# Output of the recurrence: row tiles in passes of 4 and 4, sums of squares on TensorE, one inverse root ahead of two norms

## Chip, core and metric

The kernel runs on one core of a Trainium2 chip. The metric is the device time of one execution in microseconds. TensorE multiplies, ScalarE (ACT), VectorE (DVE) and GpSimd (POOL) do the rest, SyncE issues transfers. Each engine executes its own list of instructions in order; an instruction that waits holds up all behind it on its engine. TensorE runs at one of two levels, 1.2 and 2.4 GHz; the profile prints the granted clock as a share of the higher.

## What is computed

A block of two layers (attention, then a recurrent layer of a wkv scan beside a long convolution) on 1024 tokens of width 1024, a root-mean-square norm over its output, and a second block that begins with a norm of its own and a wide input product. What the change touches is the end of the recurrent layer and the two norms in a row:

```python
def rms_norm(x, gain):
    y = x * lax.rsqrt(jnp.mean(x * x, axis=-1, keepdims=True) + 1e-6)
    return y * gain
def rwkv_readout(y, r, k_bonus, v, r_k, gn_w, gn_b):       # group norm of the scan's output per head
    mean = jnp.mean(y, axis=-1, keepdims=True)
    var = jnp.mean(jnp.square(y - mean), axis=-1, keepdims=True)
    yn = (y - mean) * lax.rsqrt(var + 64e-5) * gn_w + gn_b
    return yn + jnp.sum(r * k_bonus * r_k, axis=-1, keepdims=True) * v
# end of rec_layer
y = jnp.concatenate([y_rw * silu(g_rw), y_hy * silu(g_hy)], axis=-1) @ w_out
x = x + gate * y
# end of the first block, start of the second
x = rms_norm(x, final_norm)
h = rms_norm_2(x, g_mix) @ w_in
```

## The kernel before

Activations lie transposed: width on the partitions in 8 tiles of 128 rows, tokens along the free axis in two halves of 512. A float32 product is three reduced-precision matmuls: both operands are split into a rounded part and a remainder (hi, lo), and hi x hi, lo x hi and hi x lo are added up in one PSUM bank. For weights `wblock` does this for each output row tile: a transfer into wf (two buffers), whi on ACT (L273), wlo on DVE or POOL as `self.wlo` says (L274). `dense` runs over the output row tiles m and the token halves and issues the matmuls (L291); a list ks names the row tiles k of the input that take part. `evac` or `evac2` takes a finished bank; what they yield is called again after the next product group. `tick` is called once per product group.

The output product of the recurrence (`rec_layer`, weights rec_w_out) has 8 input row tiles k: in the order of this kernel 0 to 2 and 5 come from the convolution, 3, 4, 6 and 7 from the scan; 7 is the head pair (pair 3) whose scan output still has to go through `rwkv_readout`, a generator of some 24 steps that goes over the two token halves: broadcast of per-head numbers along the partitions (a transpose L245, then selection matmuls L252), mean and variance by small matmuls against a 0/1 matrix (L1878, L1906), an inverse root on DVE, and the scaling (L1895 DVE, L1896 ACT, L1897 POOL, L1898 DVE). `part` splits one row tile (yhi on ACT L412, ylo on DVE L413).

The first pass takes k = 0 to 4 for all m and both halves, adds into x3T (L1968) and ticks the readout one step per product group. Then the rest of the readout runs, row tiles 5 to 7 are split, and the second pass takes k = 5 to 7 for the first half. Its `evac2` adds into x3T (L1972) and calls `squares`: ACT squares the row tile (L359), POOL adds it into x3sq (L360), and DVE adds it, weighted by the square of final_norm, into x3sqg (L366). With both sums at hand, `mix_norm` makes the inverse roots for the two norms at once: four matmuls against ones add up the partitions (`mean_square`, L373), r1 is the inverse root of the first mean, r2 that of the weighted mean times r1 squared, and their product is broadcast over the partitions (`rbc`, L390, copied by ACT L392). `modulate` multiplies (L400 DVE), rounds (L402 ACT) and takes the remainder (L403, DVE or POOL). Then come the second pass of the other half and its `mix_norm`, in block 2, and block 2's input product.

The order on each engine is not that of the code: a scheduler simulates the program and decides it, and tile pools decide what may overlap. So products of one stage stand among those of the next: 48 products of block 2's input on the first half stand ahead of the second half's broadcast.

Of the kernel before, what the change touches and what calls it, by code (L numbers as in the profile page):

```python
# [11 lines left out]
F32 = mybir.dt.float32  # L12
# [129 lines left out]
class Kern:  # L142
# [207 lines left out]
    def squares(self, p, acc, t0, n, x, m, gained=None):  # L350
# [10 lines left out]
        if gained is not None:  # L361
            g, gain = gained[0][:, sl], gained[1]
            if m == 0:
                nc.vector.tensor_scalar(g, sq, gain, None, OP.mult)
            else:
                nc.vector.scalar_tensor_tensor(g, sq, gain, g, OP.mult, OP.add)  # L366
# [666 lines left out]
class KernB(Kern):  # L1033
# [887 lines left out]
    def rec_layer(self, xT, acc, close_x, pools, open_x, d_x, d_out, ahead):  # L1921
# [35 lines left out]
        xo, acc, accg = open_x()  # L1957
        with self.pool(name="b3y", bufs=1) as q:
# [11 lines left out]
            def evac2(m, gi, t0, n, ps):  # L1970
                x = xo[:, m, t0:t0 + n]
                nc.vector.scalar_tensor_tensor(x, ps[:, :n], mod[:, 16 + m, 0:1], x, OP.mult, OP.add)  # L1972
                self.squares(q, acc, t0, n, x, m, (accg, g2[:, m:m + 1]))
                if t0:
                    self.st.dma_start(d_out[m * 128:(m + 1) * 128, :], xo[:, m, :])

            g2 = self.t(self.cst, [128, 8], F32, "fn2")
            nc.vector.tensor_tensor(g2, self.c("final_norm"), self.c("final_norm"), OP.mult)
# [9 lines left out]
            for k in second:  # L1988
                part(k)
# [3 lines left out]
            ahead(xo, acc, accg, *(self.t(s, [128, 8, 512], F32R, n) for s, n in ((yps, "yH"), (yqs, "yB"))), tmp, self.t(q, [128, 1284], F32, "ush2", bufs=1)[:, :512])  # L1993
            self.dense(A["rec_w_out"], list(range(8)), yhi, ylo, LAT[1:], evac2, ks=second)
        self.wlo = nc.vector
        return (wp, yq, yp), (yps, yqs)
# [69 lines left out]
class KernC(KernB):  # L2066
# [507 lines left out]
    def mix_norm(self, x, acc, accg, t0, tmp, rb, hi, lo):  # L2574

        nc = self.nc
        r1 = self.r1[:, t0 // 128:t0 // 128 + 4]
# [176 lines left out]
```

## Time and profile before

| | us |
|---|---|
| median of 3 runs | 4241.47 (4241.17 to 4248.0) |
| the profiled execution: time | 4248.29 |
| its span | 4246.3 |
| TensorE busy | 3869.0 (91%) |
| DVE busy | 2661.3 (63%) |
| ACT busy | 1897.4 (45%) |
| POOL busy | 1231.6 (29%) |
| first rec_w_out product to the second half's broadcast | 2398.91 to 2552.65 |

The mean granted clock was 0.953. The shares are averages over stages with different limits; the change touches a stretch of some 160 us, which is read by windows and timelines of its own. In a timeline a row's "[0.34 <-POOL wlo L274]" says that the engine stood idle for 0.34 us before it and what released it. Neighbouring matmuls overlap, so the time that a matmul takes from the stream is the distance between starts, not the duration in its row.

### The profile page before, as it was taken

The page shows a single profiled execution, that of the slowest core. Times are in us where ns is not written, and L with a number is a line of the kernel's source. Part 1 is how long each engine was busy: PE and PEld are TensorE (multiplying, and loading weights), DVE is VectorE, ACT ScalarE, POOL GpSimd, SP SyncE. Part 2 cuts the span into 40 slices and gives each one's busy share as a digit, 9 for nine tenths or more (in the row PEclk, how much of TensorE's full clock was granted, in tenths as well). Part 3 has the DMA queues.
Part 4 walks back from the last instruction along what each step waited for, and adds up shares of the span by engine and source line. Part 5 has one row for each costly group of instructions (what it writes and reads, how often), then busy time and mean ns, then how long its engine had stood idle before and what let it go on. Part 6 is the DMA issues. An engine that isn't in the chain of part 4 may idle for free. (4 is left out here: it accounts for less than half of the span.)

```text
span 4246.3 us, 68831 instructions
## 1 busy us (share of the span) xinstructions
PE 3869.0 (91%) x25613; PEld 3186.3 (75%) x25613; DVE 2661.3 (63%) x5485; ACT 1897.4 (45%) x4210; POOL 1231.6 (29%) x1300
## 2 busy tenths in 40 slices
PE   7989997899999988968999879989988897999999
PEld 4778886777787767757888757878867786888787
DVE  6741525798834678756673265699777868665532
ACT  6433415777724545415667523334327433333321
POOL 4522302333333533322111043122212126544200
PEclk9999998999999999979999989999999998999999
DMA  6454316431233655564444323324345351222422
GB/s 207 154 177 161 131 70 183 103 90 31 74 119 99 181 147 171 165 163 124 125 121 113 116 88 102 112 87 141 107 128 135 132 179 52 85 80 84 152 102 73
DMA packets 388598, 516.56 MB, mean 122 GB/s; under 512 B 171751, under 2 KB 264823, under 8 KB 386600
## 3 DMA queue, kind: packets, MB, share of 16 engines
q1 hardware_dynamic: 369448, 441.38, 33.9%
q0 software_dynamic: 14064, 53.48, 3.7%
q10 hardware_dynamic: 4752, 17.30, 1.3%
q8 instruction: 202, 3.31, 0.3%
q14 instruction: 132, 1.08, 0.1%
HBM read 348.74 MB, written 164.63 MB: 121 GB/s over the span
## 5 line engine op out<-in xcount | busy, mean ns | idle before, releaser
L291 PE MATMUL bank<-hhi,whi 128*128 128x512 f32 (+1 forms) x1264 | 486.2, 385 | 12.5 <-ACT hhi L405 10.2
L291 PE MATMUL bank<-hlo,whi 128*128 128x512 f32 (+1 forms) x1264 | 483.6, 383 | 3.6 <-DVE hlo L406 1.9
L291 PE MATMUL bank<-hhi,wlo 128*128 128x512 f32 (+1 forms) x1264 | 481.8, 381 | 0.0
L273 ACT ACTIVATE whi<-wf 128x1024 fp32r<-128x1024 f32 (+3 forms) x202 | 193.7, 960 | 455.1 <-PE bank L291 391.3
L274 POOL TENSOR_TENSOR wlo<-wf,whi 128x1024 fp32r<-128x1024 f32 (+1 forms) x96 | 217.0, 2261 | 521.8 <-ACT whi L273 489.6
L291 PEld LDWEIGHTS bank<-hhi,whi 128*128 128x128 f32 x1264 | 243.3, 193 | 60.2 <-ACT hhi L405 11.0
L291 PEld LDWEIGHTS bank<-hlo,whi 128*128 128x128 f32 x1264 | 242.9, 192 | 54.0 <-DVE hlo L406 4.4
L291 PEld LDWEIGHTS bank<-hhi,wlo 128*128 128x128 f32 x1264 | 242.4, 192 | 46.0
L2495 PE MATMUL bank<-th,wh 128*128 128x512 f32 x616 | 246.5, 401 | 6.9 <-ACT th L2420 6.9
L2495 PE MATMUL bank<-th,wl 128*128 128x512 f32 x616 | 247.0, 401 | 0.0
L328 POOL TENSOR_TENSOR walo<-wa,wahi 128x512 fp32r<-128x512 f32 x96 | 130.6, 1375 | 245.2 <-ACT wahi L327 241.6
L417 POOL CAST phi<-split 128x512 fp32r<-128x512 f32 (+1 forms) x104 | 62.8, 604 | 457.9 <-ACT split L416 369.3
L291 PE MATMUL bank<-yT,whi 128*128 128x512 f32 (+1 forms) x600 | 192.9, 390 | 0.9 <-ACT rb L392 0.5
L413 DVE TENSOR_TENSOR plo<-bank,phi 128x512 fp32r<-128x512 f32 (+2 forms) x260 | 167.0, 653 | 37.6 <-ACT phi L412 36.4
L412 ACT ACTIVATE phi<-bank 128x512 fp32r<-128x512 f32 (+2 forms) x260 | 144.5, 568 | 57.1 <-PE bank L730 29.3
L291 PE MATMUL bank<-yH,whi 128*128 128x512 f32 x376 | 153.3, 408 | 11.4 <-ACT ev_a L2158 7.9
L291 PE MATMUL bank<-yB,whi 128*128 128x512 f32 x376 | 151.8, 404 | 7.5 <-DVE yB L403 6.7
L274 DVE TENSOR_TENSOR wlo<-wf,whi 128x1024 fp32r<-128x1024 f32 (+2 forms) x106 | 118.5, 1121 | 54.3 <-ACT whi L273 54.2
L291 PE MATMUL bank<-yH,wlo 128*128 128x512 f32 x376 | 151.8, 404 | 0.8 <-POOL wlo L274 0.7
L2495 PE MATMUL bank<-tl,wh 128*128 128x512 f32 x352 | 142.4, 405 | 5.6 <-DVE tl L2421 4.7
L704 ACT ACTIVATE P<-S,mx 128x768 f32<-128x768 f32 (+7 forms) x144 | 118.2, 822 | 64.9 <-DVE mx L700 58.9
L2495 PEld LDWEIGHTS bank<-th,wh 128*128 128x128 f32 x616 | 117.8, 191 | 37.0 <-ACT th L2420 8.7
(633 smaller groups left out, 11319.7 us busy)
## 6 DMA issues: line engine op xcount, KB each, us to landing
wf<-in_w_in_dram SPq DMA_DIRECT2D x47, 512.0 KB, 3.4
wf<-in_w_ffn_in_dram SPq DMA_DIRECT2D x44, 512.0 KB, 3.6
d_rec<-r_rec SPq DMA_DIRECT2D x40, 512.0 KB, 2.7
wf<-in_rec_w_in_dram ACTq DMA_DIRECT2D x33, 512.0 KB, 4.2
wf<-in_attn_w_in_dram SPq DMA_DIRECT2D x26, 512.0 KB, 3.8
wa<-in_attn_ada_w_dram POOLq DMA_DIRECT2D x24, 512.0 KB, 3.9
wa<-in_rec_ada_w_dram POOLq DMA_DIRECT2D x24, 512.0 KB, 4.1
LK<-d_rec SPq DMA_DIRECT2D x64, 192.0 KB, 3.5
```

What stands on the lines that cost most here:

```text
L273: nc.scalar.activation(hi, wf, AF.Copy)
L274: self.wlo.tensor_tensor(lo, wf, hi, OP.subtract)
L291: self.mark = nc.tensor.matmul(ps[:, :n], w[:, k - k0, :], x(k, t0, n), start=(k == ks[0] and j == 0), stop=(k == ks[-1] and j == 2))
L328: nc.gpsimd.tensor_tensor(lo[:, k], w3[:, k], hi[:, k], OP.subtract)
L412: nc.scalar.activation(hi, src, AF.Copy)
L413: nc.vector.tensor_tensor(lo, src, hi, OP.subtract)
L417: nc.gpsimd.tensor_copy(hi, full)
L704: nc.scalar.activation(P[:, :at], S[:, :at], AF.Exp, bias=m[:, i:i + 1], scale=-1.0, accum_out=st["rs"][:, bi, u["h"]:u["h"] + 1])
L2495: self.mark = nc.tensor.matmul(ps, w[i][:, k, :], x[i][k], start=(k == 0 and j == 0), stop=(k == kh - 1 and j == 2))
```

## The change

- The passes take k = 0 to 3 and 4 to 7 (before: 0 to 4 and 5 to 7). `tick` runs two steps of the readout and also calls `part` for tiles 4, 5 and 6 at its turns 5, 8 and 11; `part(7)` comes after the readout.
- The running sums x3sq and x3sqg are gone. After its Square, `evac2` yields; when it is called again, four small matmuls (L1975 in the changed kernel) take the squared row tile as stationary operand, 128 tokens each, against two columns: ones and the square of final_norm. Their bank of 128 x 8 is added into a small total per half on DVE (L1977; L1979 copies the first one).
- `mix_norm` reads both means from that total. The product of the two inverse roots is taken as one: r2 = 1/root(weighted mean + 1e-6 (mean + 1e-6)). The root r1 is still made, for a later use, behind the modulate in the code.

```diff
-    def squares(self, p, acc, t0, n, x, m, gained=None):
+    def squares(self, p, acc, t0, n, x, m):
...
-        if gained is not None:
-            g, gain = gained[0][:, sl], gained[1]
-            if m == 0:
-                nc.vector.tensor_scalar(g, sq, gain, None, OP.mult)
-            else:
-                nc.vector.scalar_tensor_tensor(g, sq, gain, g, OP.mult, OP.add)
...
-        xo, acc, accg = open_x()
+        xo = open_x()
+        sums = [self.t(self.cst, [128, 4, 2], F32, f"x3s{i}") for i in range(2)]
...
             def evac2(m, gi, t0, n, ps):
-                x = xo[:, m, t0:t0 + n]
+                x, total = xo[:, m, t0:t0 + n], sums[t0 // 512]
                 nc.vector.scalar_tensor_tensor(x, ps[:, :n], mod[:, 16 + m, 0:1], x, OP.mult, OP.add)
-                self.squares(q, acc, t0, n, x, m, (accg, g2[:, m:m + 1]))
+                sq = self.t(q, [128, 512], F32, "sumsq", bufs=2)
+                nc.scalar.activation(sq, x, AF.Square)
                 if t0:
                     self.st.dma_start(d_out[m * 128:(m + 1) * 128, :], xo[:, m, :])
+                yield
+                pq = self.bank("o", (128, 4, 2))
+                for i in range(4):
+                    nc.tensor.matmul(pq[:, i, :], sq[:, i * 128:(i + 1) * 128], g2[:, m, :], start=True, stop=True)
+                if m:
+                    nc.vector.tensor_tensor(total, total, pq, OP.add)
+                else:
+                    nc.vector.tensor_copy(total, pq)
...
+            first, second = [0, 1, 2, 3], [4, 5, 6, 7]
+            turn = 0
 
             def tick():
-                ro[:] = [g for g in ro if next(g, 0) is None]
-            first, second = [0, 1, 2, 3, 4], [5, 6, 7]
+                nonlocal turn
+                for _ in range(2):
+                    ro[:] = [g for g in ro if next(g, 0) is None]
+                turn += 1
+                if turn in (5, 8, 11):
+                    part({5: 4, 8: 5, 11: 6}[turn])
             for k in first:
                 part(k)
             self.dense(A["rec_w_out"], list(range(8)), yhi, ylo, LAT, evac, ks=first, tick=tick)
             while ro:
                 tick()
-            for k in second:
-                part(k)
+            part(7)
...
-        v = self.mean_square(acc[:, t0:t0 + 512], 4, f"c_v{t0}")
-        self.rsqrt(r1, v, 4)
-        r2 = self.mean_square(accg[:, t0:t0 + 512], 4, f"c_r2{t0}", 0.0)
-        nc.vector.tensor_tensor(r2, r2, r1, OP.mult)
-        nc.vector.tensor_tensor(r2, r2, r1, OP.mult)
-        nc.vector.tensor_scalar(r2, r2, 1e-6, None, OP.add)
+        v = self.t(self.cst, [128, 4], F32, f"c_v{t0}")
+        r2 = self.t(self.cst, [128, 4], F32, f"c_r2{t0}")
+        nc.vector.tensor_scalar(v, total[:, :, 0], 1.0 / 1024, 1e-6, OP.mult, OP.add)
+        nc.vector.tensor_scalar(r2, total[:, :, 1], 1.0 / 1024, None, OP.mult)
+        nc.vector.scalar_tensor_tensor(r2, v, 1e-6, r2, OP.mult, OP.add)
         self.rsqrt(r2, r2, 4)
-        nc.vector.tensor_tensor(r2, r2, r1, OP.mult)
         self.rbc(r2, 4, rb)
         self.modulate(tmp, x, t0, 512, rb, lambda k: self.gg[:, k:k + 1], None, lambda k: hi[:, k], lambda k: lo[:, k])
-
-    def mix_ahead(self, x, acc, accg, hi, lo, tmp, rb):
+        self.rsqrt(r1, v, 4)
```

POOL, second pass of the first half, before: the weight remainders (wlo) and the running sum x3sq.

```order
L274 TENSOR_TENSOR wlo_27462<-wf_27459,whi_27461 128x384
L274 TENSOR_TENSOR wlo_27483<-wf_27480,whi_27482 128x384
L360 TENSOR_TENSOR x3sq_26924<-x3sq_26924,sumsq_27455 128x512
L274 TENSOR_TENSOR wlo_27504<-wf_27501,whi_27503 128x384
L360 TENSOR_TENSOR x3sq_26924<-x3sq_26924,sumsq_27476 128x512
L274 TENSOR_TENSOR wlo_27525<-wf_27522,whi_27524 128x384
```

From the third row on the two kinds alternate, one of each per row tile.

The same place on POOL now; the first and third row belong to the readout (L1891 is L1897 before).

```order
L1891 TENSOR_TENSOR yB_18658<-yB_18658,r_X_5824_26978 128x512
L274 TENSOR_TENSOR wlo_27375<-wf_27372,whi_27374 128x512
L1891 TENSOR_TENSOR yB_18658<-yB_18658,r_X_5824_26978 128x512
L274 TENSOR_TENSOR wlo_27397<-wf_27394,whi_27396 128x512
L274 TENSOR_TENSOR wlo_27425<-wf_27422,whi_27424 128x512
L274 TENSOR_TENSOR wlo_27453<-wf_27450,whi_27452 128x512
```

The adds into x3sq are gone, and the remainders stand one behind the other.

TensorE, the first half's broadcast of the inverse root (L390) among products of the second half, before; each of those products reads yhi or ylo.

```order
L291 MATMUL bank_5982_27787<-yhi_26929,wlo_27784 128x512
L291 MATMUL bank_5987_27809<-yhi_26929,whi_27805 128x512
L291 MATMUL bank_5987_27809<-ylo_26930,whi_27805 128x512
L390 MATMUL bank_5946_27635<-ident_66,c_r_5943_27616 128x128 x4
L291 MATMUL bank_5987_27809<-yhi_26929,wlo_27806 128x512
L291 MATMUL bank_5987_27809<-yhi_26929,whi_27805 128x512
L291 MATMUL bank_5987_27809<-ylo_26930,whi_27805 128x512
```

The broadcast stands inside a row tile of the second half.

On TensorE now the broadcast is L384; L1975 are the small matmuls on the squares.

```order
L291 MATMUL bank_5976_27729<-yhi_26929,wlo_27726 128x512
L1975 MATMUL bank_5977_27742<-fn_5817_26931,sumsq_27720 128x2 x4
L384 MATMUL bank_5951_27620<-ident_66,c_r_5948_27603 128x128 x4
L291 MATMUL bank_5988_27787<-yhi_26929,whi_27783 128x512
L291 MATMUL bank_5988_27787<-ylo_26930,whi_27783 128x512
L1975 MATMUL bank_5983_27771<-fn_5817_26931,sumsq_27749 128x2 x4
L291 MATMUL bank_5988_27787<-yhi_26929,wlo_27784 128x512
```

Small matmuls on squares stand on both sides of the broadcast; that ahead of it belongs to the second half already, since the two halves' row tiles overlap.

TensorE, the second half's broadcast, before, with the last products of block 2 on the first half ahead of it; hhi and hlo are block 2's input of the second half.

```order
L291 MATMUL bank_6064_28094<-yB_27586,whi_28090 128x512
L291 MATMUL bank_6064_28094<-yH_27585,wlo_28091 128x512
L373 MATMUL bank_6028_27907<-ones_74,x3sqg_26925 128x1 x4
L373 MATMUL bank_6024_27887<-ones_74,x3sq_26924 128x1 x4
L390 MATMUL bank_6032_27931<-ident_66,c_r_6029_27912 128x128 x4
L291 MATMUL bank_6051_28029<-hhi_27881,whi_27987 128x512
L291 MATMUL bank_6051_28029<-hlo_27882,whi_27987 128x512
```

The two groups of sums stand directly ahead of the broadcast, and the next products read what follows from it.

On TensorE now (the last group of small matmuls on squares, L1975, stands 30 rows ahead of the broadcast):

```order
L291 MATMUL bank_6078_28137<-yH_27596,wlo_28134 128x512
L291 MATMUL bank_6078_28137<-yH_27596,whi_28133 128x512
L291 MATMUL bank_6078_28137<-yB_27597,whi_28133 128x512
L291 MATMUL bank_6078_28137<-yH_27596,wlo_28134 128x512
L384 MATMUL bank_6044_27961<-ident_66,c_r_6041_27944 128x128 x4
L291 MATMUL bank_6065_28072<-hhi_27937,whi_28030 128x512
L291 MATMUL bank_6065_28072<-hlo_27938,whi_28030 128x512
```

The sums stood directly ahead of the broadcast; now 29 products stand between the last sum and it.

## Rows read from the trace of the kernel before

**Rows 1.** Windows of the stretch: busy us (instructions) per engine, clock, DMA share, GB/s.

```profile
2399.00:2460.00 61.00, 59.83 (x269) 48.97 (x269) 26.00 (x48) 9.04 (x20) 2.62 (x3) 0.98 0.26 96
2460.00:2481.00 21.00, 12.72 (x46) 9.86 (x47) 10.36 (x23) 5.25 (x10) 5.20 (x5) 0.67 0.09 28
2481.00:2514.00 33.00, 25.93 (x112) 18.23 (x111) 25.78 (x48) 11.46 (x20) 24.15 (x19) 1.00 0.38 124
2514.00:2537.00 23.00, 14.53 (x54) 10.06 (x53) 21.17 (x19) 9.93 (x16) 17.52 (x10) 0.88 0.52 183
2537.00:2557.00 20.00, 12.46 (x52) 10.28 (x52) 10.02 (x34) 2.02 (x4) 2.74 (x6) 0.67 0.00 1
```

**Rows 2.** Timeline, TensorE, first pass: start, us, what, [idle before <-releaser].

```profile
2398.91 0.79 PE L291 MATMUL bank<-yhi,whi 128*128 128x512 f32 x1 [3.40 <-ACT whi L273]
...
2402.72 0.50 PE L291 MATMUL bank<-yhi,wlo 128*128 128x512 f32 x1 [0.38 <-DVE wlo L274]
```

**Rows 3.** Timeline, TensorE, inside the first pass.

```profile
2439.69 0.39 PE L291 MATMUL bank<-yhi,wlo 128*128 128x512 f32 x1
...
2442.18 0.39 PE L291 MATMUL bank<-yhi,wlo 128*128 128x512 f32 x1
2442.41 0.95 PE L1906 MATMUL bank<-sel,ush 128*128 128x2 f32 x8
2443.22 0.49 PE L291 MATMUL bank<-yhi,whi 128*128 128x512 f32 x1
2443.54 0.40 PE L291 MATMUL bank<-ylo,whi 128*128 128x512 f32 x1
```

**Rows 4.** Timeline, TensorE, end of the readout.

```profile
2460.12 0.67 PE L252 MATMUL bank<-bc_r,selr 128*128 128x128 f32 x4 [0.37 <-ACT bc_r L247]
...
2463.40 0.95 PE L1906 MATMUL bank<-sel,ush 128*128 128x2 f32 x8
2467.33 0.37 PE L245 MATMUL bank<-identr,chl 128*128 128x128 f32 x1 [2.98 <-DVE chl L243]
2468.07 1.11 PE L252 MATMUL bank<-bc_r,selr 128*128 128x128 f32 x4 [0.37 <-ACT bc_r L247]
2473.96 1.22 PE L291 MATMUL bank<-yhi,whi 128*128 128x512 f32 x2 [4.78 <-ACT yhi L412]
```

**Rows 5.** Timeline, TensorE, second pass of the first 512 tokens.

```profile
2485.69 0.50 PE L291 MATMUL bank<-yhi,wlo 128*128 128x512 f32 x1 [0.34 <-POOL wlo L274]
...
2488.36 0.50 PE L291 MATMUL bank<-yhi,wlo 128*128 128x512 f32 x1 [0.31 <-POOL wlo L274]
...
2513.55 1.31 PE L390 MATMUL bank<-ident,c_r 128*128 128x128 f32 x8 [1.90 <-DVE c_r L2585]
...
2516.36 0.63 PE L291 MATMUL bank<-yhi,whi 128*128 128x512 f32 x1
2516.79 0.63 PE L291 MATMUL bank<-ylo,whi 128*128 128x512 f32 x1
```

**Rows 6.** Groups from 2474 to 2557: count, busy, mean ns, idle before.

```profile
L360 POOL TENSOR_TENSOR x3sq<-x3sq,sumsq 128x512 f32<-128x512 f32 x14 | 22.5, 1609 | 3.7 <-ACT sumsq L359 3.1 <-DVE x3sqg L364 0.4
...
L366 DVE SCALAR_TENSOR_TENSOR x3sqg<-sumsq,fn,x3sqg 128x512 f32<-128x512 f32 x14 | 19.5, 1396 | 3.7 <-ACT sumsq L359 3.3
...
L274 POOL TENSOR_TENSOR wlo<-wf,whi 128x384 fp32r<-128x384 f32 x14 | 14.5, 1042 | 16.3 <-ACT whi L273 16.3
L1972 DVE SCALAR_TENSOR_TENSOR x3T<-bank,rec_mod,x3T 128x512 f32<-128x512 f32 x16 | 11.9, 745 | 3.3 <-PE bank L291 3.2
...
L359 ACT ACTIVATE sumsq<-x3T 128x512 f32<-128x512 f32 x14 | 8.7, 631 | 11.9 <-DVE x3T L1972 7.0 <-DVE x3sqg L366 4.7
...
L233 DVE TENSOR_TENSOR rq_t<-rq_i,c_r 128x4 f32<-128x4 f32 x6 | 1.0, 162 | 0.2
```

**Rows 7.** Timeline, TensorE, the second half's inverse root.

```profile
2552.65 2.08 PE L390 MATMUL bank<-ident,c_r 128*128 128x128 f32 x8 [5.41 <-DVE c_r L2585]
```

**Rows 8.** Timeline, TensorE, block 2's input products.

```profile
2536.72 0.80 PE L291 MATMUL bank<-yB,whi 128*128 128x512 f32 x1 [4.69 <-DVE yB L403]
```

More of the change, by code (lines that the diff above doesn't have):

```diff
@@ L1992, in rec_layer @@
             tmp = lambda k: self.t(q, [128, 1024], F32, ("r_U2", "r_X2", "r_U3", "r_X3")[k % 4], bufs=1)[:, :512]
-            ahead(xo, acc, accg, *(self.t(s, [128, 8, 512], F32R, n) for s, n in ((yps, "yH"), (yqs, "yB"))), tmp, self.t(q, [128, 1284], F32, "ush2", bufs=1)[:, :512])
+            ahead(xo, sums, *(self.t(s, [128, 8, 512], F32R, n) for s, n in ((yps, "yH"), (yqs, "yB"))), tmp, self.t(q, [128, 1284], F32, "ush2", bufs=1)[:, :512])
             self.dense(A["rec_w_out"], list(range(8)), yhi, ylo, LAT[1:], evac2, ks=second)
         self.wlo = nc.vector
-        return (wp, yq, yp), (yps, yqs)
+        return (wp, yq, yp), (yps, yqs), sums
 PERM = np.array([half * 32 + b * 16 + i for b in range(2) for half in range(2) for i in range(16)])
@@ L2572, in ffn_out, with mix_norm, mix_ahead @@
             k0 += nk
-    def mix_norm(self, x, acc, accg, t0, tmp, rb, hi, lo):
+    def mix_norm(self, x, sums, t0, tmp, rb, hi, lo):
         nc = self.nc
-        r1 = self.r1[:, t0 // 128:t0 // 128 + 4]
-        v = self.mean_square(acc[:, t0:t0 + 512], 4, f"c_v{t0}")
-        self.rsqrt(r1, v, 4)
-        r2 = self.mean_square(accg[:, t0:t0 + 512], 4, f"c_r2{t0}", 0.0)
-        nc.vector.tensor_tensor(r2, r2, r1, OP.mult)
-        nc.vector.tensor_tensor(r2, r2, r1, OP.mult)
-        nc.vector.tensor_scalar(r2, r2, 1e-6, None, OP.add)
+        r1, total = self.r1[:, t0 // 128:t0 // 128 + 4], sums[t0 // 512]
+        v = self.t(self.cst, [128, 4], F32, f"c_v{t0}")
[3 more added lines that the diff above has]
+        nc.vector.scalar_tensor_tensor(r2, v, 1e-6, r2, OP.mult, OP.add)
         self.rsqrt(r2, r2, 4)
-        nc.vector.tensor_tensor(r2, r2, r1, OP.mult)
         self.rbc(r2, 4, rb)
         self.modulate(tmp, x, t0, 512, rb, lambda k: self.gg[:, k:k + 1], None, lambda k: hi[:, k], lambda k: lo[:, k])
-    def mix_ahead(self, x, acc, accg, hi, lo, tmp, rb):
+        self.rsqrt(r1, v, 4)
+    def mix_ahead(self, x, sums, hi, lo, tmp, rb):
         self.r1 = self.t(self.cst, [128, 8], F32, "c_r1")
@@ L2593, in mix_ahead, with block2 @@
         self.h0 = {0: [hi, lo]}
-        self.mix_norm(x, acc, accg, 0, tmp, rb, *self.h0[0])
-    def block2(self, x, acc, accg, close_x, pools, stores, d_x, out):
+        self.mix_norm(x, sums, 0, tmp, rb, *self.h0[0])
+    def block2(self, x, sums, close_x, pools, stores, d_x, out):
         nc, tc, A = self.nc, self.tc, self.A
@@ L2616, in block2 @@
             with self.pool(name="c0", bufs=1) as p:
-                self.mix_norm(x, acc, accg, 512, lambda k: self.t(p, [128, 512], F32, "mtmp", bufs=3), self.t(p, [128, 512], F32, "rb"), *h[512])
+                self.mix_norm(x, sums, 512, lambda k: self.t(p, [128, 512], F32, "mtmp", bufs=3), self.t(p, [128, 512], F32, "rb"), *h[512])
             xhi, xlo = (lambda k, t0, n, j=j: h[t0][j][:, k] for j in range(2))
@@ L2730, in open_x3 @@
             p = st["p3"].__enter__()
-            st["x3"] = K.t(p, [128, 8, 1024], F32, "x3T"), K.t(p, [128, 1024], F32, "x3sq"), K.t(p, [128, 1024], F32, "x3sqg")
+            st["x3"] = K.t(p, [128, 8, 1024], F32, "x3T")
             return st["x3"]
-        pools, stores = K.rec_layer(*st["x1"], close(st["p1"]), pools, open_x3, d_x1, d_x3, K.mix_ahead)
-        K.block2(*st["x3"], close(st["p3"]), pools, stores, d_x3, out)
+        pools, stores, sums = K.rec_layer(*st["x1"], close(st["p1"]), pools, open_x3, d_x1, d_x3, K.mix_ahead)
+        K.block2(st["x3"], sums, close(st["p3"]), pools, stores, d_x3, out)
 def kernel(**inputs):
```

5 lines of the change are left out of this document (3 added, 2 removed).

## The prediction

> **What bounds the kernel now.** I read the chain that ended last first: the output products of the recurrence and their helpers stand on it, so a microsecond saved there is a microsecond of the span, if nothing later waits for something else. Then the windows of that stretch [rows 1], and for each window with idle TensorE its timeline with the releaser of each wait. The stretch runs from the first rec_w_out product at 2398.91 us [rows 2] to the broadcast of the second half's inverse root at 2552.65 [rows 7]: 153.7 us. The first window is full (59.83 of 61 us, clock 0.98); the other four hold 65.6 us of TensorE busy time in 97 us, two of them at a mean clock of 0.67 [rows 1].
>
> At full clock one product follows another by 2.49/11 = 0.2266 us (2439.69 to 2442.18, rows 3). There are 384 rec_w_out products in the stretch (16 groups, 8 row tiles, 3 products), and 48 of block 2's input ordered into it: 432 x 0.2266 = 97.9 us. The readout's own TensorE work there is 6 broadcast groups at 0.67 [rows 4] and 2 groups of small sums at 0.90 (0.81 to the next product, which then takes 0.32 instead of 0.2266, rows 3): 5.8. Four groups of L373, as long as that group of eight small passes: 3.2; the first L390 at about 1.0 (half of the second's 2.08, which ran at the low clock, rows 7). Together **107.9**; the other **45.8 us are waits and half clock**, in four places:
> - The readout ends late: its last broadcasts stand behind 12 products of the second pass, and TensorE then idles 2.98 for the inverse root and 4.78 for the split of row tile 7 [rows 4]; the products that follow start at the low clock.
> - In the second pass of the first half every row tile waits for POOL's wlo: its period is 2.67 us (2485.69 to 2488.36, rows 5) where 9 products need 2.04. POOL does one x3sq add (1.609) and one wlo (1.042) per row tile [rows 6]: 2.65, so POOL is the bound there.
> - L390 of the first half waits 1.90 for DVE's two inverse roots [rows 5], and the products after it come at 0.43 spacing (2516.36, 2516.79), the clock's low level. One product of block 2 then waits 4.69 for the modulate on DVE [rows 8], an engine that also carries 14 weighted accumulations of 1.396 [rows 6].
> - After the last products nothing is left to do: two groups of sums, 28 dependent small DVE operations, then L390, which waited 5.41 [rows 7].
>
> **Part by part.** *The 4 and 4 split* neither adds nor removes products: the first pass has 192 instead of 240, the second 192 instead of 144. It moves one row tile from the shorter part to the part behind the readout, and so gives the readout 48 products (10.9 us) less to hide behind. *Two readout steps per turn* answers that: before, some 24 steps at one per turn of 15 products (3.40 us); now 12 turns of 12 products (2.72 us) = 33 of the pass's 43.5 us. In the new order the last broadcast stands 177 products from the start instead of 252, with 24 products behind it and the second pass's row tiles 4 to 6 ahead of the split of tile 7. The tail from that broadcast to the first product on tile 7 took 5.9 us (2468.07 to 2473.96, rows 4); 24 products cover 5.4, so I leave some 0.5 there and about 1.9 for places where a broadcast or a bank stands at the head of the queue: **2.4**, where before 2.98 and 4.78 and a half-clock start stood. Splits of tiles 4 to 6 are called at turns 5, 8 and 11, but their inputs are ready from the start, and in the new order all seven still stand ahead of the first whi on ACT: that edit moves nothing, and in any case DVE is busy 26.0 of 61 us there and ACT 9.0 [rows 1].
>
> *The start.* The first product waits for ACT's whi [rows 2], behind the same seven splits. Ahead of the first product with wlo stand 6 products instead of 8 (three groups' first two), so the wait there grows from 0.38 [rows 2] by two products at the low level (0.43 each, rows 5) to 1.2; with the products at half clock (about 13 x 0.20): **3.9** at the start, and my guess of 1.85 inside the pass for banks and the denser readout.
>
> *Sums on TensorE.* Removed: 14 POOL adds of 1.609 (22.5 us), 14 DVE accumulations of 1.396 (19.5), four groups of L373 (3.2). Added: 16 groups of four small matmuls in eight passes. Their form (a 128x128 stationary block, 2 columns) is that of L1906, which costs 0.90 of TensorE's time [rows 3]: 16 x 0.90 = **14.4 us on the path**, and 16 DVE adds of 128x8 at 0.16 like other small ones [rows 6], 2.6, beside the products. A row tile of the second pass then takes 12 x 0.2266 + 0.90 = 3.62 us on TensorE, against POOL's wlo of 512 columns (1.042 x 512/384 = 1.39), ACT's Square of 0.631 and a whi of about that length and DVE's x3T (0.745) plus 0.16. No other engine is near it: POOL's bound goes, and 3.62 for four row tiles stands where 2.67 for three stood. The new groups stand two row tiles behind their Square in the queue, so they wait for nothing; if they waited, all products behind them would. After the first half one place remains: row tile 5's whi waits for tile 3's products, which the scheduler put late, then its wlo follows: **2.0**. Ends for a group: nothing, if small passes hide in the stream, and 1.9, if each waits one microsecond; I take 0.90, since the nearest row measures that form.
>
> The Trainium skill's page "TensorE: Matmul & The Clock Gate", section "Back-to-back issue gap", gives about 25 ns for an isolated matmul of 1 to 64 columns, and warns that it leaves out the weight load; by it, as an estimate, a group of eight costs 0.2 us, all of them 3.2, and the time would be 11 us lower. The 0.81 of the row speaks against it.
>
> *One inverse root.* The chain to the broadcast had 28 small operations in 5.41 us [rows 7], 0.19 each; now it needs the add, three operations for v and r2, and 11 of one root, but the order interleaves r1's 11 on DVE, so 26 remain between sums and broadcast: 4.9. What changes is the place: in the new order 29 products (6.6 us) lie between the last group of sums and the second L384. So the 5.41 goes, L384 starts at full clock and takes about 1.0 instead of 2.08. The first L384 has 22 products and two groups of sums ahead of it (6.8 us), so its 1.90 goes too, and the low clock behind it; one x3T of 0.745 among the small operations fits into either, and a wait of up to 1 there is part of the range. The 4.69 at the modulate [rows 8] goes because DVE and POOL no longer have the accumulations in front of it, and 60 products lie between the first broadcast and block 2's first. What follows the second broadcast (copy, modulate, split) keeps its order and is shifted as a whole.
>
> **The sum.** 107.9 - 3.2 + 14.4 = 119.1 of work; waits 3.9 + 1.85 + 2.4 + 2.0 = 10.1; 129.2 instead of 153.7, so the second broadcast comes 24.5 earlier, plus about 1.0 from its clock: 25.5, rounded to **25**. The rows are from an execution of 4248.29 us (span 4246.3), 6.8 above the median of 4241.47; the stretch is not where such a difference needs to lie, so I take the gain from the median: **4216.5 us**. Its own range: waits of 4 us instead of 10.1 (the start alone) give -31, waits of 18 (a low clock for some 40 products) -17: 4210 to 4224.
>
> **Rivals.**
> - *The readout is still late (B).* Two steps per turn only help if a step's inputs are there. It is some 14 dependent links per half, each queued behind an x3T of 0.745 or a wlo on DVE; at 1 us of queueing per link (28 us beside some 32 of bare chain) it overruns the 48 us of the pass by about 12, TensorE idles and starts at the low clock. Gain 13: 4228. For it: 24 products of cover against a tail of 5.9. Against it: engines beside TensorE are half idle in that window [rows 1].
> - *The sums wait (C).* If each of the 16 groups stands 1 us at TensorE's head for its Square or bank: 16 less, gain 8 to 9, 4233. It decides where a Square ends over 3.2 us (14 products) after its row tile; x3T and Square take 1.4 [rows 6].
> - *Small passes hide (E).* A group costs 0.3 or the waits are all absent: 8 to 10 more, 4207.
> - *Slower: the second pass falls to the low clock (D).* It is now 16 times cut by small groups. At 0.43 instead of 0.2266 a product costs 0.20 more; 192 products: 38, less 25, 13 slower: 4255. From 123 products at the low level the gain is gone, from 165 it is slower by over 0.2%. For it: after idle times of 1.90 and 4.78 the clock fell [rows 4, 5]. Against it: the windows from 2481 to 2514 had a clock of 1.00 with a wait of 0.3 in every row tile [rows 1, 5]. The same page, section "A second HAM failure mode: psum-queue depth-cycling", tells of a clock that swings where TensorE idles shortly between groups of products; it would make D more likely, but those rows do not show it for waits of 0.3.
> - The change not doing what it says (the order keeping the old place of the second broadcast) is excluded by the order of instructions.
>
> **How the numbers follow.** Forecast 0.56, E 0.09, B 0.17, C 0.10, D 0.08. 0.2% is 8.5 us, about what a measurement of this kernel tells from no change; faster by more: forecast, E, nearly all of B (0.16) and half of C (0.05) = 0.86; within: rest of B and C and the mild part of D, 0.07; slower: 0.07. The range takes in the forecast's ends, E and B's deeper side: **4205 to 4231**; most of C and D are left out, about 0.17.
>
> **What would show it.** TensorE idles no more than 1 us at a time between the last readout broadcast and the second pass; row tiles of the second pass about 3.6 us apart with POOL idle between its wlos; groups of small sums 0.8 to 0.9 and no wait on a Square; the wait before the second broadcast under 0.5 and its start near 2528; clock near 1.00 from 2405 to 2528. The prediction is wrong if the clock falls in the second pass, if the readout leaves a gap of 5 us, or if the part after the second broadcast has grown, which is shifted as a whole in my sum.

## The result: 36 us by the medians, and more than the stretch explains

The changed kernel takes 4205.22 us (median of 4, 4202.1 to 4208.1), the one before 4241.32 (median of 4, 4239.5 to 4248.0). The ratio is 0.9898, 95% interval 0.9882 to 0.9914: 1.0% less, or 43 us with an interval of 36 to 50. The medians of this comparison differ by 36, at the low edge of that interval; a second comparison gave 0.9892 (0.9878 to 0.9907), and there the medians lie 43 apart (4252.73 and 4210.00). The profiled execution took 4202.55 us, its span 4200.8. Forecast were 25 us less. The direction is right, the amount is not: the forecast was for 0.6%, and even its deep end (36) stands only at the interval's edge.

The prediction's stretch, from the first rec_w_out product (2395.07 in this trace) to the second half's broadcast (2523.79), lasted 128.72 us: forecast were 129.2, before it was 153.7. So the total held where it was made; its terms are checked further down. These are the windows over the stretch, changed kernel (us; busy us and instructions of TensorE, its weight loads, DVE, ACT, POOL; clock, DMA share, GB/s); they answer to [rows 1].

```profile
2395.00:2450.00 55.00, 52.09 (x233) 41.75 (x234) 27.27 (x61) 9.64 (x22) 3.19 (x3) 0.95 0.27 102
2450.00:2490.00 40.00, 39.35 (x208) 32.97 (x207) 15.96 (x48) 14.23 (x22) 15.10 (x12) 1.00 0.25 91
2490.00:2524.00 34.00, 33.06 (x178) 27.97 (x177) 20.18 (x51) 13.22 (x21) 16.98 (x13) 1.00 0.53 180
```

TensorE is busy 124.5 of 129 us, the clock is 1.00 after the first window, and POOL's 24.15 of 33 us [rows 1] are 15.10 of 40 in the second pass. Now TensorE's timeline around the end of the readout, which answers to [rows 4, 5]:

```profile
2438.98 0.50 PE L291 MATMUL bank<-yhi,whi 128*128 128x512 f32 x1 [1.04 <-DVE yB L1880]
...
2446.40 0.28 PE L245 MATMUL bank<-identr,chl 128*128 128x128 f32 x1 [0.68 <-DVE chl L243]
2447.05 0.66 PE L252 MATMUL bank<-bc_r,selr 128*128 128x128 f32 x4 [0.37 <-ACT bc_r L247]
...
2453.77 0.50 PE L291 MATMUL bank<-yhi,whi 128*128 128x512 f32 x1 [0.23 <-ACT whi L273]
...
2455.45 0.50 PE L291 MATMUL bank<-yhi,wlo 128*128 128x512 f32 x1 [0.41 <-POOL wlo L274]
...
2458.30 0.95 PE L1975 MATMUL bank<-fn,sumsq 128*128 128x2 f32 x8
2459.12 0.48 PE L291 MATMUL bank<-yhi,wlo 128*128 128x512 f32 x1
...
2461.95 0.95 PE L1975 MATMUL bank<-fn,sumsq 128*128 128x2 f32 x8
```

The wait of 2.98 us in [rows 4] is 0.68. That of 4.78 for the split of row tile 7 is gone; where the second pass begins, TensorE waits 0.23 and 0.41 for weights. A row tile of the second pass lasts 3.65 us (2458.30 to 2461.95; forecast 3.62), and eight small passes are 0.82 until the next product. The wait for row tile 5's weights and the second broadcast, which answers to [rows 7]:

```profile
2505.35 0.50 PE L291 MATMUL bank<-yhi,whi 128*128 128x512 f32 x1 [0.94 <-ACT whi L273]
...
2523.79 1.06 PE L384 MATMUL bank<-ident,c_r 128*128 128x128 f32 x8
2527.03 0.51 PE L291 MATMUL bank<-hhi,whi 128*128 128x512 f32 x1 [2.19 <-ACT hhi L396]
...
2538.53 1.05 PE L1900 MATMUL bank<-sel,ev_b 128*128 128x2 f32 x8
```

The broadcast (L384) waits for nothing (5.41 before) and lasts 1.06 (2.08 before). The first product behind it starts 3.24 us after it, 4.21 before: 0.97, the 1.0 of the sum. Two things that the sum lacked follow. First, group L1900 at 2538.53 lasts 1.05 here, and the same group before, behind the product that ends the wait of 2.13, lasted 1.70:

```profile
2556.86 0.80 PE L291 MATMUL bank<-hhi,whi 128*128 128x512 f32 x1 [2.13 <-ACT hhi L402]
...
2569.94 1.70 PE L1906 MATMUL bank<-sel,ev_b 128*128 128x2 f32 x8
```

TensorE stood at its low level there, but not still from the waits of 5.41 and 2.13: windows of the kernel before show the high level in between.

```profile
2563.00:2568.00 5.00, 3.89 (x14) 1.77 (x12) 2.85 (x5) 3.16 (x6) 2.45 (x4) 1.00 0.32 91
2570.00:2575.00 5.00, 5.00 (x17) 4.29 (x16) 3.11 (x11) 1.17 (x3) 3.09 (x2) 0.50 0.34 123
```

And in a second trace of the same kernel (e1 below) the same waits stand ahead of the group, and it runs at the high level:

```profile
2552.05 2.08 PE L390 MATMUL bank<-ident,c_r 128*128 128x128 f32 x8 [5.41 <-DVE c_r L2585]
2556.26 0.80 PE L291 MATMUL bank<-hhi,whi 128*128 128x512 f32 x1 [2.13 <-ACT hhi L402]
...
2568.95 0.96 PE L1906 MATMUL bank<-sel,ev_b 128*128 128x2 f32 x8
```

So the second fall belongs to the single execution. Between the traces the offset is -3.8 us at the stretch's first product (the scan ahead of it, which the change does not touch; in all the traces this product starts between 2393 and 2408), -28.9 at the second broadcast, -32.5 at the product that starts at 2572.51 before: 3.6 behind the broadcast, of which 1.0 was forecast and most of the rest is that fall. Second, the offset then grows, not evenly, to -45.5 at the end of the span, for the most part in places where no engine is waited for in either trace. The feed-forward output, some 1450 us behind the change, shows it: before and after, a window of 100 us wholly filled with products.

```profile
4000.00:4100.00 100.00, 100.00 (x429) 80.39 (x428) 42.78 (x61) 23.48 (x35) 0.00 (x0) 1.00 0.40 143
```

```profile
3960.00:4060.00 100.00, 100.00 (x438) 82.08 (x437) 43.44 (x62) 23.24 (x35) 0.00 (x0) 1.00 0.40 146
```

429 matmuls before, 438 after, at the same clock, with no idle time. Nothing in the diff touches this code.

### The profile page after: what moved, and what is told of

The parts are those of the page before. It is cut to its first block, busy times and chain, and to the rows that moved or that the text cites. A ratio compares the mean times of both kernels' runs of the same rounds, so it can differ in the third digit from the quotient of the medians.

```text
span 4200.8 us, 69009 instructions
## 1 busy us (share of the span) xinstructions
PE 3845.9 (92%) x25709; PEld 3186.2 (76%) x25709; DVE 2638.4 (63%) x5479; ACT 1897.0 (45%) x4210; POOL 1212.8 (29%) x1287
## 4 chain that ended last, share of the span: by engine, by line
PE 65%; DVE 18%; ACT 6%; DMA 5%; issue 3%; SPq 2%; POOL 1%; ACTq 0%; DVEq 0%; POOLq 0%
PE bank L291 33%; PE bank L2505 10%; PE bank L2405 2%; PE bank L856 2%; PE bank L884 1%; PE bank L724 1%; DVE r_X L1655 1%; PE bank L685 1%; PE bank L1195 1%; PE bank L1329 1%; DVE ush L1653 1%; DVE S L694 1%; PE bank L879 1%; PE bank L334 1%; PE bank L880 1%
## 5 line engine op out<-in xcount | busy, mean ns | idle before, releaser
L274 DVE TENSOR_TENSOR wlo<-wf,whi 128x1024 fp32r<-128x1024 f32 (+3 forms) x106 | 117.5, 1111 | 53.0 <-ACT whi L273 52.9
L291 PE MATMUL bank<-yB,whi 128*128 128x512 f32 x376 | 149.2, 397 | 0.0
```

Source lines behind the costliest of these rows:

```text
L274: self.wlo.tensor_tensor(lo, wf, hi, OP.subtract)
L291: self.mark = nc.tensor.matmul(ps[:, :n], w[:, k - k0, :], x(k, t0, n), start=(k == ks[0] and j == 0), stop=(k == ks[-1] and j == 2))
```

## Experiments: the distance of products goes with where tiles begin

Joining the traces with the addresses of the compiled programs shows what differs. The constants' pool lies at the bottom of SBUF; the totals and the wider table of gains (fn2) make it 96 bytes per partition larger, so all pools on the left, with the weights of most products, begin at 30368 instead of 30272. Pools on the right, with most moving tiles, stay. (The x3T pool lost 8 KB too; e3 tests that.) I sorted the distances of 512-column products (from the start of the one ahead, high clock, no wait; means by form of product) by where both operands begin, modulo 512:

| weights, moving (before) | mean us | weights, moving (after) | mean us |
|---|---|---|---|
| 64, 480 (yH, yB, hhi, fh, th) | 0.2337 to 0.2344 | 160, 480 | 0.227 to 0.232 |
| 480, 64 (yT, yhi) | 0.231 to 0.238 | 480, 160 | 0.2335 |
| 64, 64 (hhi) | 0.2280 | 160, 160 | 0.2280 |
| 480, 480 (mhi) | 0.2272 | 480, 480 | 0.2270 |

The theory: operands that begin alike follow at 0.227 to 0.228, others more slowly, by some 3% on average in the kernel before. The rivals: the single execution, the room left free, the changed work.

**e1, e2: both kernels once more.** No edit.

> The kernel before, once more, for a second trace of it. Of the 45.5 us between the two traces' spans, 25.0 arise between the first rec_w_out product and the second broadcast, 4 in the 70 us behind it, and some 12.5 as a slow drift behind that, where products follow at 0.2345 us before and 0.2300 after with no idle time in either. If that drift is a matter of the single execution, this trace shows other distances in that stretch (0.229 to 0.235) and its time differs from 4248.3 by as much as the distances explain; if it belongs to the kernel, it shows 0.2345 again. Time 4238 to 4249, ratio to before 1.000 within 0.002.

> The changed kernel, once more. If the slow drift is a matter of the single execution, distances of products behind 2600 us lie between 0.229 and 0.235, and the gain over before is 33 to 40 us; if it belongs to the kernel, distances are 0.2300 again and the gain is 40 or more.

Ratios 0.9994 (0.9985 to 1.0003) and 0.9892 (0.9878 to 0.9907). The same kind of window, before and after:

```profile
4005.00:4105.00 100.00, 100.00 (x429) 80.38 (x428) 42.16 (x61) 23.33 (x35) 0.00 (x0) 1.00 0.41 146
```

```profile
3960.00:4060.00 100.00, 100.00 (x439) 82.04 (x438) 42.56 (x61) 23.25 (x35) 0.00 (x0) 1.00 0.41 143
```

429 again, and 439 after 438: it belongs to the kernel, not to the execution. Other things do differ between executions: from the second broadcast to the end of the span are 1693.7 us before and 1698.3 in e1, 1677.0 in the changed kernel and 1681.0 in e2. So such a time tells differences of more than some 5 us.

**e3: the room of the accumulators kept.**

```diff
             st["x3"] = K.t(p, [128, 8, 1024], F32, "x3T")
+            for n in ("x3sq", "x3sqg"):
+                K.nc.gpsimd.memset(K.t(p, [128, 1024], F32, n)[:, :1], 0.0)
```

> The changed kernel, with the two accumulators x3sq and x3sqg (8 KB per partition) still in their pool, unused but for a one-column fill each, so that what is placed behind them lies where it lay before. If the drift comes from where the later tiles lie, the distances are 0.2345 again and it is 8 to 13 us slower than the changed kernel; if not, it is within 3 us of it, some 4203 to 4208.

Ratio 0.9904 (0.9891 to 0.9916), 5 us more than e2 by the ratios and within their intervals; in the window 438 matmuls:

```profile
3970.00:4070.00 100.00, 100.00 (x438) 82.05 (x438) 42.59 (x61) 23.26 (x35) 0.00 (x0) 1.00 0.42 143
```

The freed 8 KB are not it.

**e5: the kernel before, 96 bytes further.** The only edit is a spare tile among the constants (416 bytes in e8; 320 in e7, on the changed kernel):

```diff
         iwc = self.t(self.cst, [128, 8, 4], F32, "iwc")
+        nc.gpsimd.memset(self.t(self.cst, [128, 24], F32, "spare")[:, :1], 0.0)
```

> The kernel before, with nothing changed but 96 spare bytes per partition among the constants: the same number by which the change's totals and its table of gains grow that pool, so that all pools on the left of SBUF begin at 30368 as in the changed kernel instead of 30272, while those on the right stay. In the traces of both kernels the distance of two products goes with where the weights and the moving tile begin, taken modulo 512: 0.2344 us at weights 64, moving 480; 0.230 at 160 and 480; 0.227 where both are equal. Theory of the address: distances behind 2600 us fall from 0.2345 to 0.230, the stretch of the change keeps its 152 to 154 us, and it is 10 to 18 us faster than before. Rival, that the drift belongs to the changed work: 0.2345 and the same time within 3 us.

Ratio 0.9960 (0.9947 to 0.9973), 17 us less, with one small fill more and all else the same:

```profile
3980.00:4080.00 100.00, 100.00 (x439) 82.04 (x438) 42.40 (x61) 23.58 (x36) 0.00 (x0) 1.00 0.42 149
```

The stretch is 153.15 us, that of before; from the second broadcast to the end of the span are 1677.2 us (1693.7 before, 1677.0 in the changed kernel). The 96 bytes alone give the whole drift, as far as such a time can tell.

**e6: the changed kernel at the old place.**

```diff
-        sums = [self.t(self.cst, [128, 4, 2], F32, f"x3s{i}") for i in range(2)]
+        sums = [self.t(self.xp, [128, 4, 2], F32, f"x3s{i}") for i in range(2)]
...
-            g2 = self.t(self.cst, [128, 8, 2], F32, "fn2")
+            g2 = self.t(self.xp, [128, 8, 2], F32, "fn2")
```

> The changed kernel, with totals and table of gains in the pool of x3T (filled up to 512 bytes with a spare tile) and 32 spare bytes among the constants, so that all left pools begin at 30272 as before. Theory of the address: the stretch stays at 128.8 us, the distances behind it are 0.2345 again, and 10 to 16 us of the gain are lost: a gain of 27 to 33 over before, that of the work alone (25.0 in the stretch, 4 just behind it, up to 3 elsewhere). Rival: the time of the changed kernel, a gain of 40 to 46.

Two spare tiles, not shown, belong to the edit: one of 32 bytes among the constants keeps the left pools at 30272, one of 384 fills up the pool of x3T. Ratio 0.9949 (0.9932 to 0.9967): 22 us less than before (14 to 29), below the expected 27 to 33 in its middle. Stretch 128.66, 1693.8 from its end to that of the span, and

```profile
3970.00:4070.00 100.00, 100.00 (x429) 80.38 (x428) 42.07 (x61) 22.60 (x35) 0.00 (x0) 1.00 0.40 143
```

So the work of the change is worth 22 by this comparison, with an interval that holds the forecast's 25, and the rest of its gain is the place.

**e7 and e8: both kernels with left and right alike.**

> The changed kernel with 320 spare bytes per partition among the constants, so that left pools begin at 30688, which modulo 512 is 480 like the right ones: weights and moving tiles of nearly all products then begin alike. Theory of the address: distances of 0.227 in the block 2 products, in the feed-forward part and in the first layer's products, some 4600 of them 3.2 ns and 2000 of them 6.6 ns shorter: 20 to 28 us faster than the changed kernel, a gain of 60 to 72 over before. Rival, that only the place by itself counts and not that both are alike: within 5 us of the changed kernel.

> The kernel before with 416 spare bytes among the constants: left pools begin at 30688 too, alike with the right ones. Theory of the address: 4600 products 7.3 ns and 2000 products 6.6 ns shorter, 35 to 47 us faster than before, and more than the whole change brought; the changed kernel with the same start then leads it by the 27 to 33 us of the work alone. Rival: within 5 us of before.

e7 has 0.9854 (0.9840 to 0.9868), 4192.02 us beside 4252.59: 62 less, some 18 below the changed kernel; e8 0.9918 (0.9904 to 0.9931), 4218.95: 35 less with the old work. Both came out at the low end of what was expected or somewhat under it, and e7 leads e8 by 26.9 by the medians, the work alone. Their windows, e7 first:

```profile
3945.00:4045.00 100.00, 100.00 (x442) 82.79 (x442) 42.65 (x61) 23.28 (x35) 0.00 (x0) 1.00 0.41 143
```

```profile
3965.00:4065.00 100.00, 100.00 (x443) 82.78 (x442) 42.48 (x61) 23.57 (x36) 0.00 (x0) 1.00 0.43 152
```

442 and 443 matmuls in 100 us, and the distances in these windows are 0.2267 on average (0.2343 in that of before, 0.2289 in that of the changed kernel). e7 beats both kernels, and is the fastest that was run.

**e13 to e15: what alike means.** The spare tile of e5 with 160, 288 and 352 bytes puts left and right 256, 128 and 64 bytes apart modulo 512.

> The kernel before with 160 spare bytes among the constants: left pools begin at 30432, 224 modulo 512, 256 apart from the right ones (480). If starts count as alike modulo 256, distances of products behind 2600 us are 0.227 and the time is that with 416 spare bytes (some 35 us less than before); if only modulo 512, they are 0.229 to 0.235 and it is 0 to 20 us faster than before.

> The kernel before with 288 spare bytes: left pools at 30560, 352 modulo 512, 128 apart. Alike modulo 128: 0.227 and 35 us less than before; else 0.229 to 0.235 and 0 to 20 us less.

> The kernel before with 352 spare bytes: left pools at 30624, 416 modulo 512, 64 apart. Alike modulo 64: 0.227 and 35 us less than before, but 320 apart, a multiple of 64, was slower already, so 0.229 to 0.235 and 0 to 20 us less are more likely.

Windows of e13, e14, e15:

```profile
3985.00:4085.00 100.00, 100.00 (x443) 82.79 (x442) 42.91 (x62) 23.26 (x35) 0.00 (x0) 1.00 0.41 146
```

```profile
3985.00:4085.00 100.00, 100.00 (x432) 81.08 (x431) 42.60 (x61) 23.27 (x35) 0.00 (x0) 1.00 0.41 143
```

```profile
3985.00:4085.00 100.00, 100.00 (x439) 82.05 (x438) 42.14 (x61) 23.48 (x35) 0.00 (x0) 1.00 0.41 143
```

443 with 256 bytes between them, 432 and 439 with 128 and 64. Starts count as alike modulo 256. The feed-forward output of e15 (416, which is 160 modulo 256) has the mean distance of e5, 0.2289. It is a mean of three forms of product at 0.2267, 0.2291 and 0.2310; which form has which differs between traces of the same placing (e5 and e15 too), so the starts fix the mean of the stream and not the distance of one form. The ratios are 0.9927 (0.9895 to 0.9959), 0.9985 (0.9966 to 1.0004) and 0.9988 (0.9965 to 1.0011); in that comparison the executions scattered more, and by their times e14 and e15 are not told from the kernel before; e15 has the distances of e5 but not its ratio of 0.9960. So I go by the windows and by the time from the second broadcast to the end: 1665.6, 1681.6 and 1677.2 us. Only the left pools were moved in all these runs; that it is the distance between both starts, and not the place of the left pools alone, rests on the rows of the table where both lie elsewhere and alike (64 with 64, 160 with 160). Why the distance of products depends on it is not shown by these runs.

## Experiments: the parts of the work

These are compared by the stretch from first product to second broadcast, which does not hang on the place (152.2 to 154.2 in seven traces of the old work, mean 153.6; 128.6 to 129.8 in five of the new, mean 128.9).

**e4: the passes and the readout alone.** The kernel before with the diff's new `tick`, `first` and `second`.

> The kernel before with the 4 and 4 split, two readout steps per turn and splits of tiles within the pass, but with the running sums on POOL and DVE and the two inverse roots as before. By the prediction's sum it mends the end of the readout (8.9 us of waits there to 2.4, and the half clock behind it, some 4) and, with 12 products per row tile (2.72 us), nearly covers POOL's adds of 1.6 and remainders of 1.39 (3.0); the second broadcast still waits 5.4. Gain 8 to 14 us of 25 in the stretch: 4228 to 4234. The rival, that sums on POOL bind harder now (3.0 per row tile against 2.72): 16 x 0.3 = 5 less, 4233 to 4239.

Ratio 0.9955 (0.9940 to 0.9969), 19 us less; stretch 138.0, so 15.6 of it.

```profile
2459.50 0.28 PE L245 MATMUL bank<-identr,chl 128*128 128x128 f32 x1 [0.68 <-DVE chl L243]
...
2466.88 0.50 PE L291 MATMUL bank<-yhi,whi 128*128 128x512 f32 x1 [0.23 <-ACT whi L273]
...
2546.24 2.07 PE L390 MATMUL bank<-ident,c_r 128*128 128x128 f32 x8 [5.41 <-DVE c_r L2591]
```

The readout's waits are 0.68 and 0.23 as in the changed kernel; the 5.41 at the broadcast stays. It beat the expected 8 to 14.

**e9: the passes of before in the changed kernel.** The reverse edit.

> The changed kernel with the passes of before: row tiles 0 to 4 and 5 to 7, one readout step per turn, tiles 5 to 7 split behind it; sums on TensorE and one inverse root stay. The first pass then ends as before: its last broadcast behind 12 products of the second pass, waits of 2.98 and 4.78 and the half clock behind them. The split alone brought 14 to 15 us of the stretch (153 to 138.0), so if the parts add up, this stretch is 129 + 14 to 15 = 143 to 144 us. Rival: the small sums and the shorter second pass gain more where three row tiles are left (POOL's bound of 2.67 against 2.94), or less, since 21 products stand before the second broadcast instead of 29: 139 to 149. Left pools begin at 30368 as in the changed kernel, so the rest is 1677 to 1681 us behind the broadcast.

Stretch 138.6, 9.7 more than in the changed kernel, where 143 to 144 were expected; ratio 0.9931 (0.9915 to 0.9946). TensorE's waits (what waited, for whom: us, times, longest):

```profile
PE bank L291 <- ACT yhi L406: 4.8, 1, 4.8
...
PE bank L245 <- DVE chl L243: 3.0, 1, 3.0
```

Both waits of [rows 4] are back. The 9.7 lie under what was expected, and 138.6 just under the rival's 139 to 149 as well. The passes bring 15.6 on the old work and 9.7 with the sums and the one root there, these 15.0 and 9.1: together 24.7, 5.9 less than the two alone. What both remove was not taken apart.

**e11: one readout step per turn.**

```diff
-                for _ in range(2):
-                    ro[:] = [g for g in ro if next(g, 0) is None]
+                ro[:] = [g for g in ro if next(g, 0) is None]
```

> The changed kernel with one readout step per turn instead of two. The last broadcast of the readout then stands behind 210 products, 18 into the second pass, instead of 177. If two steps per turn are what hides the readout, TensorE waits some 8 us for its tail and for the split of row tile 7 and starts at the low clock (3 more): stretch 138 to 141 instead of 128.8. Rival: the 4 and 4 passes alone leave room enough, and it stays within 3 us of 128.8.

Stretch 135.5, 6.6 more; ratio 0.9905 (0.9891 to 0.9920).

```profile
2456.35 0.28 PE L245 MATMUL bank<-identr,chl 128*128 128x128 f32 x1 [2.98 <-DVE chl L243]
2457.00 1.11 PE L252 MATMUL bank<-bc_r,selr 128*128 128x128 f32 x4 [0.37 <-ACT bc_r L247]
```

The 2.98 at the inverse root is back, and the broadcast behind it lasts 1.11 instead of 0.66. So two steps are needed, as said, at a somewhat smaller price than I gave (138 to 141). The time alone does not tell this kernel from the changed one.

**e10: one inverse root alone**, on the kernel before; r1 moves behind the modulate.

```diff
-        nc.vector.tensor_tensor(r2, r2, r1, OP.mult)
-        nc.vector.tensor_tensor(r2, r2, r1, OP.mult)
-        nc.vector.tensor_scalar(r2, r2, 1e-6, None, OP.add)
+        nc.vector.scalar_tensor_tensor(r2, v, 1e-6, r2, OP.mult, OP.add)
         self.rsqrt(r2, r2, 4)
-        nc.vector.tensor_tensor(r2, r2, r1, OP.mult)
```

> The kernel before with one change: the product of the two inverse roots taken as one, the root r1 behind the modulate; passes, readout and running sums as before. By the prediction's reading, 12 of 28 small operations leave the chain ahead of each broadcast: at 0.19 each 2.3 us at the second, and most of the 1.9 at the first with some half clock behind it: stretch 148.5 to 151 instead of 152.2 to 153.7, gain 2 to 5 us. Rival: the scheduler interleaves r1's operations on DVE, so that the chain is as long as before: no gain.

Ratio 0.9991 (0.9981 to 1.0000), 4 us less (at most 8); stretch 145.0, 8.6 less, more than expected.

```profile
2549.32 2.08 PE L390 MATMUL bank<-ident,c_r 128*128 128x128 f32 x8 [2.63 <-DVE c_r L235]
```

The second broadcast waits 2.63 instead of 5.41: 2.78 less. That is 14 links less in the chain of DVE operations ahead of it, but only 3 operations less: the 11 of r1 still stand there, one by one between those of r2. A step of both roots together takes what a step of one took before, 0.20 us (e10, then the kernel before):

```profile
2548.13 0.16 DVE L233 TENSOR_TENSOR rq_t<-rq_i,c_r 128x4 f32<-128x4 f32 x1
2548.21 0.15 DVE L233 TENSOR_TENSOR rq_t<-rq_i,c_v 128x4 f32<-128x4 f32 x1
2548.32 0.24 DVE L234 SCALAR_TENSOR_TENSOR rq_t<-rq_t,rq_i 128x4 f32<-128x4 f32 x2
```

```profile
2551.25 0.16 DVE L233 TENSOR_TENSOR rq_t<-rq_i,c_r 128x4 f32<-128x4 f32 x1
2551.45 0.16 DVE L234 SCALAR_TENSOR_TENSOR rq_t<-rq_t,rq_i 128x4 f32<-128x4 f32 x1
```

So the prediction's count of 26 operations at 0.19 (4.9) was the wrong measure; in the changed kernel the chain runs in pairs as well, and products cover it. The rest of the 8.6 lies ahead of the first broadcast (109.4 us from the first product instead of 114.6), where the order of products is another; I did not take it apart. The trace is of the fastest of ten executions, and the times bear out no more than 8 of the 8.6.

**e12: the sums twice.**

```diff
-                for i in range(4):
+                for i in [0, 1, 2, 3] * 2:
```

> The changed kernel with each of the 16 groups of small matmuls on the squares issued twice (the second writes the same numbers again). If a group lies on TensorE's path at 0.81 to 0.90 us, the stretch grows by 16 x 0.81 = 13.0 us from 128.8 to 141 to 143, and the time by 12 to 14. Rival, that small passes hide in the stream or cost their issue alone (0.2 to 0.3 a group): 132 to 134.

Stretch 149.2, 20.3 more; ratio 0.9930 (0.9913 to 0.9946).

```profile
2457.84 1.84 PE L1975 MATMUL bank<-fn,sumsq 128*128 128x2 f32 x16
...
2462.37 1.84 PE L1975 MATMUL bank<-fn,sumsq 128*128 128x2 f32 x16
```

A row tile lasts 4.53 instead of 3.65 (2457.84 to 2462.37), so a group costs 0.88 and 16 of them 14.1: the small passes lie on the path at the price of [rows 3]. By the Trainium skill's 25 ns for an isolated small matmul ("TensorE: Matmul & The Clock Gate", section "Back-to-back issue gap") all groups together would have cost an estimated 3.2; this trace does not agree. The remaining 6 us were a surprise; windows further on in the same run:

```profile
2510.00:2515.00 5.00, 4.25 (x27) 3.08 (x25) 5.00 (x8) 3.06 (x6) 2.97 (x2) 1.00 0.48 163
2515.00:2520.00 5.00, 5.00 (x22) 4.52 (x22) 0.96 (x4) 0.91 (x2) 1.28 (x1) 0.56 0.94 325
2520.00:2525.00 5.00, 5.00 (x22) 4.61 (x21) 0.91 (x2) 1.69 (x2) 2.35 (x1) 0.50 0.38 152
```

The clock stands at its low level from 2515.6 to 2529.3, 13.7 us at half the speed, which is about the 6 us. TensorE had stood idle for no more than 0.51 us at a time in the 50 us ahead of it; just ahead stood two groups of 16 passes within 5 us. So a fall like that of rival D exists. With the change's own number of groups the clock stays at 1.00 up to the second broadcast, once it has risen behind the first products, in the changed kernel, e2, e6 and e7. In e3 it fell at the same place for 3.4 us, behind a wait of 0.93 for row tile 5's weights and two groups in a row; the changed kernel has a wait of 0.94 there without a fall. The window of e3:

```profile
2517.00:2521.00 4.00, 4.00 (x13) 3.23 (x14) 1.23 (x4) 1.58 (x3) 3.81 (x2) 0.58 0.71 247
```

That the passes by themselves bring the clock down is not shown: in e12 two groups as close together, with the first broadcast between them, stand at 2498 to 2503, and the clock stays at 1.00 there.

## Why the prediction missed, point by point

- **What bounds the kernel and the sum of the stretch: right.** 128.7 for 129.2. The row tile (3.65 for 3.62), the group of small passes (0.88 for 0.90), the readout's place, POOL's bound gone, the second broadcast without a wait: each as it was put. The smaller terms were less exact, and that they add up to within 0.5 us is in part luck. The first wlo product stands behind six others, as said, but waits 0.2 and not 1.2, and the start is worth 2.8 and not 3.9; the guess of 2.0 for row tile 5 was 0.94. In all, TensorE idles 4.4 us and loses 2.6 to the low clock at the start: 7.0, where 10.1 stood. The rest, the work, takes 121.7, where 119.1 stood.
- **"What follows the second broadcast ... is shifted as a whole": the step that failed.** The order stayed, but what follows also became shorter: 1677.0 us from the second broadcast to the end of the span instead of 1693.7, where the sum had 1.0 for the clock and nothing else. Most products behind it changed their distance, because 96 bytes more of constants moved the weights. It goes with the place and not with the work: with the left pools at 30272 this time is 1693.5 to 1698.3 in five traces of old and new work (before, e1, e4, e6, e10), at 30368 it is 1677.0 to 1681.0 in seven (the changed kernel, e2, e3, e5, e9, e11, e12). That was worth 17 us (e5) of the 43; e6 without it has 22, e7 against e8 27. The forecast of 25 was right for the work and took no account of the place. The 1.0 for the end of the half clock is there at the first product behind the broadcast (0.97), but nothing of it can be told at the end of the span: 1693.7 before and 1693.8 in e6, 1677.2 in e5 and 1677.0 in the changed kernel. Nothing in the trace of before showed a distance that depends on addresses by itself, but [rows 3] had 0.2266 and the windows of block 2 and of the feed-forward part 0.234 at the same clock, and I passed over that difference.
- **Rivals.** B was refuted by the waits of 0.68 and 0.23, and e11 shows where it begins. C: no group waited for its Square. E: e12 refutes that small passes hide; the total that it gave (4207) was met for another reason. D did not occur in the changed kernel, but e12, and e3 for 3.4 us, show how near it is. One of the two signs given for it was misread: the clock was low before the wait of 4.78, for the broadcast ahead of that wait lasted 1.11 already, where another lasted 0.67 [rows 4].
- **The range.** Its low end of 4205.0 is 36.5 below the median of before, about the upper end of the ratio's interval; it was built of the stretch's terms alone.

## To carry to other kernels

Compare the distance of equal matmuls between stages and between two kernels before explaining a difference by waits: where it differs at the same clock and with no idle time, look at where the weights and the moving tile begin. Here a few hundred spare bytes that made both begin alike modulo 256 were worth as much as a careful reordering. An edit that adds constants at the bottom of a stack of pools also moves every pool above them; try it with the place held fixed.

## What was not expected of the hardware

Distances of 512-column products by how far the starts of weights and moving tile are apart: 0.227 us where the distance is a multiple of 256 bytes, about 0.232 at 128, 0.2265 to 0.234 at 64, 0.231 to 0.238 at 160. The mean of a stream was the same in all traces of the same placing (the feed-forward output within 0.0001); one group (x, at the start of the feed-forward sums) had 0.231 with both alike at 64 modulo 256, so the rule has an exception that was not explained. And a clock that falls after small passes with idle times of 0.51 and 0.24 us (e12) or 0.93 (e3), while the second pass of the kernel before, with 0.3 idle in every row tile of products alone, keeps 1.00 [rows 1, 5].
